# Sums moved from GpSimd to VectorE, and a later place for the solved blocks, in a decoder layer

## The chip, the core and the metric

The kernel runs on one core of a Trainium2 chip. Its time is the device time of one execution in microseconds (us); what counts is the median over several executions. The core has a matrix engine (TensorE, PE in the profile), an engine for elementwise work on two operands (VectorE, DVE), one for activations and casts (ScalarE, ACT), a slower one for elementwise work and for issuing transfers (GpSimd, POOL), and a queue of transfers without arithmetic (SyncE, SP). Every engine works off its own list of instructions in order, and waits on semaphores where an instruction needs something that another engine or a transfer has not finished.

## The reference

One decoder layer on 512 tokens of width 1024, in float32. In short:

```
u    = rmsnorm(x)
proj = u @ w_in                      # q, k, v, gates of two token mixers, two merge gates
ro   = silu(rgate) * groupnorm(retention(rq, rk, rv))         # 8 heads
do   = silu(dz) * rmsnorm(gated_delta(cq, ck, cv, g, beta))   # 8 heads, chunks of 128
         # inside: solve (I + A) sol = rhs, A strictly lower triangular, 128 x 128 per chunk and head
h    = x + (sigmoid(gate_r) * (ro @ w_ret_br) + sigmoid(gate_d) * (do @ w_dn_br)) @ w_o
up   = causal_depthwise_conv(rmsnorm(h) @ w_up)
out  = rmsnorm(h + (silu(a) * b) @ w_down)                    # a, b the halves of up
```

The result has to keep float32 accuracy.

## The kernel before

**Products.** TensorE multiplies rounded float32 operands fast. For full accuracy each operand is split into a high part (a cast) and a low part (the operand less its high part), and every product is three matmuls: high by high, high by low, low by high. A weight block is 128x1024: SyncE loads it into one of four raw buffers (`wraw`, `fetch()`), ScalarE casts it (`whi`), VectorE subtracts (`wlo`), and TensorE then works on both (`weights()`, `take()`). There are four buffers each of `whi` and `wlo`. A raw buffer is free, and the next load goes out, once its `wlo` is made.

**Stages.** First come the columns of `w_in` for the mixers (`dense_c` and others), and, among them, the two mixers themselves. Then four square products 512x1024 by 1024x1024, `matrix(0)` to `matrix(3)`: the merge gates of the delta branch (0) and of the retention branch (1), then the delta branch's output (2) and the retention branch's output (3). After them `w_o` (OUT), the upward product with its convolution, and the downward product. The square products and the downward one use a seven-product scheme in place of eight: each operand is cut into quarters B11, B12, B21, B22, and sums T1 to T4 of the quarters are made on chip. The weights' sums are made by transfers that add in memory, issued by GpSimd (`presum`, `s` in the profile), each released by a pair of tiny instructions, `tick` on ScalarE and `tock` on GpSimd (`pace()`). The sums for stage 3 and OUT are issued by `late_sums()`, which starts when the last head's solve is up. In a square stage one product is two weight blocks of 12 matmuls each, in PSUM as `py`.

**Sums and ends of a stage.** `combine_c` makes T3 and T1 on GpSimd and T2 and T4 on VectorE, in four rows of 128x256, for four column groups of each operand (`uy`, `uz`, `dy`, `dz`, `ry`, `rz`). `combine()`, which other operands use, makes all four on VectorE. `u_raw()` first puts u together again from its high and low part, eight sums of 128x512 (`ur`). `parts_of` and `part_of` split a sum into high and low (`oh`, `ol`, `o`). When a stage's tile of 128x512 is complete (`ended`), `branch_end` multiplies it with its gate: in stage 2 on GpSimd, in stage 3 on VectorE, followed by an addition of the two branches (`res<-res,res` in the profile). `m_out` then transposes the merged tile on TensorE (`pmt`, L219), ScalarE copies it out, and sums for OUT are made from it (`mt`, one of them on GpSimd, `mT` after the split). Ahead of `matrix(3)` SyncE issues eight loads of x (`h`, 256 KB each) for the residual.

**The solve.** For each of two groups of four heads, `solve(g)` inverts 32x32 blocks on VectorE, stores them and loads them back in another layout by transfers (`x_dram`, then `tt`), waits, and starts `solve_up`, whose first matmuls read `tt` (`pm`, 32x32).

**What sets the order.** There is no runtime scheduler. The program is written as generators, and an `Order` object keeps a model clock: every matmul moves the clock on by its planned cost, every instruction of another engine gets a planned end from a cost function, and a generator that yields n goes on n planned microseconds after its last instruction's planned end. `poll()`, called between products, issues whatever is due. So the yields and the cost functions decide the place of each instruction in its engine's list; the lists are fixed when the kernel is built. All VectorE, ScalarE and GpSimd rows are recorded at L200, matmuls at L215.

Of the kernel before, what the change touches and what calls it, by code (L numbers as in the profile page):

```python
# [11 lines left out]
F32 = mybir.dt.float32  # L12
F32R = mybir.dt.float32r
AF = mybir.ActivationFunctionType
ALU = mybir.AluOpType
# [40 lines left out]
HK = KT // 2  # L56
# [41 lines left out]
class Order:  # L98
# [29 lines left out]
    def spawn(self, gen, after=0.0):  # L128
        self.n += 1
        heapq.heappush(self.tasks, ((self.clock if self.now is None else self.now) + after, self.n, gen))  # L130
# [91 lines left out]
def body(nc, tc, ctx, io):  # L222
    sp = nc.sync
    order = Order()
    spawn, poll, hold = order.spawn, order.poll, order.hold
    vec = Engine(order, "vec", nc.vector, vec_cost)
    act = Engine(order, "act", nc.scalar, act_cost)
    pool = Engine(order, "pool", nc.gpsimd, pool_cost)
# [14 lines left out]
    def S(name, dt=F32):  # L243
        return heap.tile([P, T], dt, name=name, tag="s", bufs=HEAP)
# [17 lines left out]
    def ck(n, f=P):  # L262
        return slice(n * f, (n + 1) * f)
# [208 lines left out]
    def halves(a):  # L472
        return a[:, ck(0, 256)], a[:, ck(1, 256)]

    def combine(raw, k, nk, y, z):

        b11, b12 = halves(raw[k])
        b21, b22 = halves(raw[k + nk])
        (t3, t1), (t2, t4) = halves(y), halves(z)
        vec.tensor_tensor(t3, b22, b12, ALU.subtract)  # L480
        vec.scalar_tensor_tensor(t2, t3, -1.0, b11, ALU.mult, ALU.subtract)
        vec.tensor_tensor(t1, b11, b12, ALU.subtract)
        vec.scalar_tensor_tensor(t4, t2, -1.0, b21, ALU.mult, ALU.subtract)
# [47 lines left out]
    def transpose4(src, name):  # L531
        pt = PS(name)
        for n in range(NT):
            pe.transpose(pt[:, ck(n)], src[:, ck(n)], ident)
        return pt
# [62 lines left out]
    uhi = [S(f"uhi{k}", F32R) for k in range(KT)]  # L598
    ulo = [S(f"ulo{k}", F32R) for k in range(KT)]
    u = (uhi, ulo)  # L600
# [255 lines left out]
    def solve(g):  # L856

        group = heads[g * GH:(g + 1) * GH]
        while not all("k" in hd["got"] for hd in group):
            yield 0.3  # L860
        while g > 0 and not all("o" in hd["got"] for hd in heads[(g - 1) * GH:g * GH]):
            yield 0.3
        sa = [heap.tile([P, 32, 16], F32, name=f"sa{i}", tag="s", bufs=HEAP) for i in range(2)]
        adv = a_dram[g].rearrange("b h n i j -> (b h n) i j")
        for i in range(2):
            sp.dma_start(sa[i][:NP], adv[:, :, ck(i, 16)])
        xx = small.tile([P, 32, 32], F32, name="xx", tag="xx", bufs=1)
        tmp = small.tile([P, 32, 32], F32, name="xtmp", tag="xtmp", bufs=1)
        pool.memset(xx[:NP], 0.0)
        pool.memset(xx.rearrange("p a b -> p (a b)")[:NP, ::33], 1.0)  # L870
        yield 8.0
        for j in range(31):
            shp = [NP, j + 1, 31 - j]
            a = sa[j // 16][:NP, j + 1:, j % 16].unsqueeze(1).to_broadcast(shp)
            tv, xv_ = tmp[:NP, :j + 1, j + 1:], xx[:NP, :j + 1, j + 1:]
            vec.tensor_tensor(tv, a, xx[:NP, :j + 1, j:j + 1].to_broadcast(shp), ALU.mult)
            vec.tensor_tensor(xv_, xv_, tv, ALU.subtract)
            yield
        sp.dma_start(x_dram[g].rearrange("b h n i j -> (b h n) (i j)"), xx[:NP].rearrange("p a b -> p (a b)"))
        for b in range(4):  # L880
            sp.dma_start(tt_all[R32[b], :, R32[b]], x_dram[g][b].rearrange("h n j i -> j (h n) i"))
        yield 11.0
        for i, hd in enumerate(group):
            spawn(solve_up(hd, i), i * 4.0)

# [268 lines left out]
    dd, rr_, uu = ({} for _ in range(3))  # L1154
# [1 line left out]
    sums_of = {}  # L1156

    def combine_c(raw, x, c):

        y, z = S(f"{x}y{c}"), S(f"{x}z{c}")  # L1160
        b11, b12 = halves(raw[c])
        b21, b22 = halves(raw[c + HK])
        (t3, t1), (t2, t4) = halves(y), halves(z)
        pool.tensor_tensor(t3, b22, b12, ALU.subtract)
        yield
        pool.tensor_tensor(t1, b11, b12, ALU.subtract)
        vec.scalar_tensor_tensor(t2, t3, -1.0, b11, ALU.mult, ALU.subtract)
        vec.scalar_tensor_tensor(t4, t2, -1.0, b21, ALU.mult, ALU.subtract)
        yield
        sums_of[x, c] = y, z  # L1170

    def gate_out(ps, c, src, raw, x):
# [9 lines left out]
    def u_raw():  # L1182
        for k in (0, 4, 1, 5, 2, 6, 3, 7):
            uu[k] = S(f"ur{k}")
            pool.tensor_tensor(uu[k], uhi[k].bitcast(F32), ulo[k].bitcast(F32), ALU.add)
            yield 3.0
            if k >= HK:
                yield from combine_c(uu, "u", k - HK)

    for k in range(HK):  # L1190
        for i, (j, t) in (("B11", (0, 0)), ("B21", (1, 0)), ("B22", (1, 1))):
# [2 lines left out]
    def parts_of(opnd, names, src):  # L1194

        hi, lo = S("oh", F32R), S("ol", F32R)
        yield from split(hi, lo, src)
        for (name, k), h, l in zip(names, halves(hi), halves(lo)):
            opnd[name, k] = h, l

    def part_of(opnd, name, k, src):
        hi, lo = halves(S("o", F32R))
        yield from split(hi, lo, src)
        opnd[name, k] = hi, lo
# [3 lines left out]
    def operands_c(opnd, raw, x, gap, since):  # L1208

        if raw:  # L1210
            for c in range(HK):
                while now[0] < since[0] or c not in raw:
                    yield 0.5
                spawn(part_of(opnd, "B11", c, raw[c][:, ck(0, 256)]))
                yield gap
            for c in range(HK):
                while now[0] < since[1] or c + HK not in raw:
                    yield 0.5
                spawn(parts_of(opnd, (("B21", c), ("B22", c)), raw[c + HK]))
                spawn(combine_c(raw, x, c))  # L1220
                yield gap
        names = ("T3", "T1"), ("T2", "T4")
        for n, i in enumerate((1, 0)):
            for c in range(HK):
                while (x, c) not in sums_of or now[0] < since[2 + n]:
                    yield 0.5
                spawn(parts_of(opnd, [(name, c) for name in names[i]], sums_of[x, c][i]))
                yield gap
# [15 lines left out]
    def all_operands():  # L1244
        yield from operands_c(u_opnd, None, "u", 1.2, (0, 0, 0, 0))
        yield from operands_c(d_opnd, dd, "d", 2.0, (8, 9, 12, 13))

    spawn(all_operands())
    spawn(operands_c(r_opnd, rr_, "r", 2.0, (14, 15, 16, 17)))
    gates = [{}, {}]  # L1250
    merged = {}


    o_raw, o_opnd = {}, {}
# [4 lines left out]
    def o_split(name, t, src):  # L1259
        hi, lo = S(f"m{name}", F32R), S(f"m{name}", F32R)  # L1260
        yield from split(hi, lo, src)
        o_opnd[name, t] = hi, lo

    def m_out(t, i, r):
        yield 0.2
        pt = transpose4(r, "pmt")
        yield
        name, half = f"B{i + 1}{t // 2 + 1}", t % 2
        m = o_raw[name, half] = S(f"mr{t}{i}")
        act.copy(m, pt)  # L1270
        yield
        if name in ("B11", "B21", "B22"):
            spawn(o_split(name, half, m))
        if name == "B12":
            t3 = S("mt3")
            vec.tensor_tensor(t3, o_raw["B22", half], m, ALU.subtract)
            t2 = o_raw["T2", half] = S("mt2")
            vec.scalar_tensor_tensor(t2, t3, -1.0, o_raw["B11", half], ALU.mult, ALU.subtract)
            spawn(o_split("T2", half, t2), 0.2)
            yield 2.5  # L1280
            t1 = S("mt1")
            pool.tensor_tensor(t1, o_raw["B11", half], m, ALU.subtract)
            yield
            spawn(o_split("T1", half, t1), 0.2)
            yield 2.5
            spawn(o_split("T3", half, t3), 0.2)
        elif name == "B21":
            yield 1.5
            t4 = S("mt4")
            vec.scalar_tensor_tensor(t4, o_raw["T2", half], -1.0, m, ALU.mult, ALU.subtract)  # L1290
            spawn(o_split("T4", half, t4), 0.2)
# [9 lines left out]
    def branch_end(s, t, i, r, ps):  # L1301
        g = gates[s - 2].pop((t, i))
        if ps is None:
            (pool if s == 2 else vec).tensor_tensor(r, r, g, ALU.mult)
        else:
            vec.scalar_tensor_tensor(r, ps, -1.0, g, ALU.mult, ALU.mult)
        if s == 2:
            merged[t, i] = r
            return
        vec.tensor_tensor(r, r, merged.pop((t, i)), ALU.add)  # L1310
        yield
        yield from m_out(t, i, r)
# [330 lines left out]
```

## Time and profile before

| | before |
|---|---|
| median of 3 runs | 1029.83 us (1029.27 to 1030.21) |
| the profiled execution's own time | 1027.94 us |
| its span, first to last instruction | 1026.1 us |
| mean granted TensorE clock | 0.989 |
| TensorE busy | 991.8 us, 97% |
| VectorE busy | 737.7 us, 72% |
| ScalarE busy | 535.6 us, 52% |
| GpSimd busy | 213.9 us, 21% |

The busy shares are means over stages. What a stage is worth is read from its own stretch of the timeline, from the waits of TensorE that fall into it, and from the clock that was granted there (1.00 is full speed). Idle time on an engine other than TensorE costs nothing by itself. Stages 2 and 3 lie between about 490 and 620 us, the first group's solve ends at 186 us.

### The profile page before, as it was taken

What the parts mean: (1) busy time and instruction counts of PE and PEld (TensorE: products, weight loads), DVE (VectorE), ACT (ScalarE), POOL (GpSimd) and SP (SyncE); (2) the same over time, 40 slices, a digit from 0 to 9 for tenths busy, and PEclk for the clock granted to TensorE, in tenths of its full rate; (3) what the DMA queues carried; (4) which work ended last, traced back from release to release, by engine and by line L of the source; (5) the groups of instructions that cost most, each with busy time, mean ns of one, the idle gap of its engine ahead of it and who ended that gap; (6) DMA issues with size and microseconds to landing.
All of it is one profiled execution on the core that took longest, in us unless ns stands there. A gap on an engine that the chain in (4) does not pass through costs nothing.

```text
span 1026.1 us, 14395 instructions
## 1 busy us (share of the span) xinstructions
PE 991.8 (97%) x5241; PEld 823.5 (80%) x5241; DVE 737.7 (72%) x1332; ACT 535.6 (52%) x1132; POOL 213.9 (21%) x252
## 2 busy tenths in 40 slices
PE   8999999999999999999997979999999999999997
PEld 7888888687778887888885767788888888888886
DVE  5867797556677796565799669966555676778785
ACT  5699222278655322576675355654443443346664
POOL 3022112114333212442333301022112212000001
PEclk9999999999999999999999989999999999999999
DMA  7243559567668623359999863646669999346663
GB/s 260 83 141 117 156 184 232 164 189 148 170 202 175 157 94 115 104 181 272 346 275 244 236 208 124 224 154 219 235 213 194 212 204 218 101 125 193 202 185 123
DMA packets 82230, 189.29 MB, mean 184 GB/s; under 512 B 22704, under 2 KB 31216, under 8 KB 82160
## 3 DMA queue, kind: packets, MB, share of 16 engines
q1 hardware_dynamic: 54640, 123.36, 36.9%
q0 software_dynamic: 27520, 65.02, 28.6%
q8 instruction: 41, 0.67, 0.3%
q14 instruction: 29, 0.24, 0.1%
HBM read 185.17 MB, written 68.19 MB: 247 GB/s over the span
## 4 chain that ended last, share of the span: by engine, by line
PE 59%; DVE 8%; DMA 4%; ACT 3%; issue 2%; POOL 0%; POOLq 0%; DVEq 0%; ACTq 0%
PE pa L215 12%; PE pb L215 12%; PE pd L215 10%; PE pz L215 8%; PE py L215 5%; DVE wlo L200 3%; DMA wraw<-s 3%; PE pv L215 2%; PE po L215 2%; PE pq L215 2%; DMA wraw<-wm 2%; PE psc L215 1%; PE pk L215 1%; DVE res L200 1%; ACT whi L200 1%
## 5 line engine op out<-in xcount | busy, mean ns | idle before, releaser
L200 DVE TENSOR_TENSOR wlo<-wraw,whi 128x1024 fp32r<-128x1024 f32 x212 | 267.6, 1265 | 71.0 <-ACT whi L200 70.6
L200 ACT CAST whi<-wraw 128x1024 fp32r<-128x1024 f32 x212 | 219.4, 1035 | 163.4 <-PE pr L215 55.7
L200 POOL TENSOR_SCALAR tock<-tick 128x1 f32<-128x1 f32 x72 | 35.6, 495 | 356.1 <-ACT tick L200 356.0
L200 DVE SCALAR_TENSOR_TENSOR acc<-pb,prm,acc 128x511 f32<-128x511 f32 (+1 forms) x44 | 33.0, 749 | 57.2 <-ACT acc L200 56.4
L215 PE MATMUL pa<-u2lo,whi 128*128 128x512 f32 (+1 forms) x192 | 71.7, 373 | 1.8 <-DVE u2lo L200 1.8
L215 PE MATMUL pa<-u2hi,whi 128*128 128x512 f32 (+1 forms) x192 | 71.6, 373 | 0.0
L215 PE MATMUL pa<-u2hi,wlo 128*128 128x512 f32 (+1 forms) x192 | 71.4, 372 | 0.0
L215 PE MATMUL py<-wlo,oh 128*128 128x512 f32 x160 | 63.9, 399 | 7.2 <-DVE wlo L200 7.2
L215 PE MATMUL pb<-u2hi,whi 128*128 128x512 f32 (+1 forms) x184 | 70.0, 380 | 0.0
L215 PE MATMUL pb<-u2lo,whi 128*128 128x512 f32 (+1 forms) x184 | 70.0, 380 | 0.0
L215 PE MATMUL pb<-u2hi,wlo 128*128 128x512 f32 (+1 forms) x184 | 70.0, 380 | 0.0
L215 PE MATMUL py<-whi,oh 128*128 128x512 f32 x160 | 64.1, 401 | 0.0
L215 PE MATMUL py<-whi,ol 128*128 128x512 f32 x160 | 63.5, 397 | 0.0
L215 PE MATMUL pd<-whi,T 128*128 128x512 f32 (+1 forms) x198 | 55.5, 366 | 0.0
L215 PE MATMUL pz<-uhi,whi 128*128 128x512 f32 x128 | 52.5, 410 | 0.0
L215 PE MATMUL pr<-whi,uhi 128*128 128x512 f32 x128 | 52.1, 407 | 0.0
L215 PE MATMUL pr<-whi,ulo 128*128 128x512 f32 x128 | 50.8, 397 | 0.0
L215 PE MATMUL pr<-wlo,uhi 128*128 128x512 f32 x128 | 50.5, 394 | 0.0
L215 PE MATMUL pz<-uhi,wlo 128*128 128x512 f32 x128 | 50.0, 391 | 0.0
L215 PE MATMUL pz<-ulo,whi 128*128 128x512 f32 x128 | 50.0, 390 | 0.0
L200 DVE SCALAR_TENSOR_TENSOR acc<-pa,prm,acc 128x511 f32<-128x511 f32 (+1 forms) x44 | 33.0, 749 | 19.0 <-ACT acc L200 18.2
L215 PEld LDWEIGHTS pa<-u2lo,whi 128*128 128x128 f32 x192 | 36.2, 188 | 8.7 <-DVE u2lo L200 2.4
(320 smaller groups left out, 2498.9 us busy)
## 6 DMA issues: line engine op xcount, KB each, us to landing
wraw<-w SPq DMA_DIRECT2D x100, 512.0 KB, 4.5
s<-wm POOLq DMA_DIRECT2D x30, 1024.0 KB, 7.5
wraw<-s SPq DMA_DIRECT2D x60, 512.0 KB, 4.3
s<-wd POOLq DMA_DIRECT2D x24, 704.0 KB, 5.5
wraw<-wm SPq DMA_DIRECT2D x30, 512.0 KB, 4.5
s<-s POOLq DMA_DIRECT2D x10, 1024.0 KB, 11.2
wraw<-wd SPq DMA_DIRECT2D x15, 512.0 KB, 3.6
s<-s POOLq DMA_DIRECT2D x8, 704.0 KB, 9.4
```

What stands on the lines that cost most here:

```text
L200: return f(out, *args, **kw)
L215: self.engine.matmul(out, lhsT, rhs, start=start, stop=stop, **kw)
```

## The change

Five edits. The pause after the `tt` transfers of a solve is 13.5 planned us in place of 11.0. `combine_c` calls `combine()`, so that T3 and T1 are made on VectorE as well, and it is no longer a generator: its four rows are issued in one go. The sums of `u_raw`, one sum of `m_out` and the gating of stage 2 go to VectorE.

```diff
--- before.py
+++ after.py
@@ -879,7 +879,7 @@
         sp.dma_start(x_dram[g].rearrange("b h n i j -> (b h n) (i j)"), xx[:NP].rearrange("p a b -> p (a b)"))
         for b in range(4):
             sp.dma_start(tt_all[R32[b], :, R32[b]], x_dram[g][b].rearrange("h n j i -> j (h n) i"))
-        yield 11.0
+        yield 13.5
         for i, hd in enumerate(group):
             spawn(solve_up(hd, i), i * 4.0)
 
@@ -1156,17 +1156,8 @@
     sums_of = {}
 
     def combine_c(raw, x, c):
-
         y, z = S(f"{x}y{c}"), S(f"{x}z{c}")
-        b11, b12 = halves(raw[c])
-        b21, b22 = halves(raw[c + HK])
-        (t3, t1), (t2, t4) = halves(y), halves(z)
-        pool.tensor_tensor(t3, b22, b12, ALU.subtract)
-        yield
-        pool.tensor_tensor(t1, b11, b12, ALU.subtract)
-        vec.scalar_tensor_tensor(t2, t3, -1.0, b11, ALU.mult, ALU.subtract)
-        vec.scalar_tensor_tensor(t4, t2, -1.0, b21, ALU.mult, ALU.subtract)
-        yield
+        combine(raw, c, HK, y, z)
         sums_of[x, c] = y, z
 
     def gate_out(ps, c, src, raw, x):
@@ -1182,10 +1173,11 @@
     def u_raw():
         for k in (0, 4, 1, 5, 2, 6, 3, 7):
             uu[k] = S(f"ur{k}")
-            pool.tensor_tensor(uu[k], uhi[k].bitcast(F32), ulo[k].bitcast(F32), ALU.add)
+            vec.tensor_tensor(uu[k], uhi[k].bitcast(F32), ulo[k].bitcast(F32), ALU.add)
             yield 3.0
             if k >= HK:
-                yield from combine_c(uu, "u", k - HK)
+                combine_c(uu, "u", k - HK)
+                yield 1.0
 
     for k in range(HK):
         for i, (j, t) in (("B11", (0, 0)), ("B21", (1, 0)), ("B22", (1, 1))):
@@ -1217,7 +1209,7 @@
                 while now[0] < since[1] or c + HK not in raw:
                     yield 0.5
                 spawn(parts_of(opnd, (("B21", c), ("B22", c)), raw[c + HK]))
-                spawn(combine_c(raw, x, c))
+                combine_c(raw, x, c)
                 yield gap
         names = ("T3", "T1"), ("T2", "T4")
         for n, i in enumerate((1, 0)):
@@ -1279,8 +1271,7 @@
             spawn(o_split("T2", half, t2), 0.2)
             yield 2.5
             t1 = S("mt1")
-            pool.tensor_tensor(t1, o_raw["B11", half], m, ALU.subtract)
-            yield
+            vec.tensor_tensor(t1, o_raw["B11", half], m, ALU.subtract)
             spawn(o_split("T1", half, t1), 0.2)
             yield 2.5
             spawn(o_split("T3", half, t3), 0.2)
@@ -1301,7 +1292,7 @@
     def branch_end(s, t, i, r, ps):
         g = gates[s - 2].pop((t, i))
         if ps is None:
-            (pool if s == 2 else vec).tensor_tensor(r, r, g, ALU.mult)
+            vec.tensor_tensor(r, r, g, ALU.mult)
         else:
             vec.scalar_tensor_tensor(r, ps, -1.0, g, ALU.mult, ALU.mult)
         if s == 2:
```

Because every generator's due time follows from planned ends, rows elsewhere move too. GpSimd's list goes from 242 to 202 rows, VectorE's from 1166 to 1212. Three places:

TensorE's list at the first solved blocks. `pr` is the weight block's product with u, `pm` the first matmuls that read `tt`. Before:

```order
L215 MATMUL pr_1847<-whi_1800,ulo4_166 128x512
L215 MATMUL pm0_1940<-tt_178,A0_630 32x32 x8
L215 MATMUL pr_1847<-whi_1800,uhi5_159 128x512
L215 MATMUL pr_1847<-wlo_1809,uhi5_159 128x512
L215 MATMUL pr_1847<-whi_1800,ulo5_167 128x512
```

In the change, from the same row on:

```order
L215 MATMUL pr_1847<-whi_1800,ulo4_166 128x512
L215 MATMUL pr_1847<-whi_1800,uhi5_159 128x512
L215 MATMUL pr_1847<-wlo_1809,uhi5_159 128x512
L215 MATMUL pr_1847<-whi_1800,ulo5_167 128x512
L215 MATMUL pr_1848<-whi_1800,uhi4_158 128x512
L215 MATMUL pr_1848<-wlo_1809,uhi4_158 128x512
L215 MATMUL pr_1848<-whi_1800,ulo4_166 128x512
L215 MATMUL pr_1848<-whi_1800,uhi5_159 128x512
L215 MATMUL pr_1848<-wlo_1809,uhi5_159 128x512
L215 MATMUL pr_1848<-whi_1800,ulo5_167 128x512
L215 MATMUL pm0_1951<-tt_178,A0_630 32x32 x8
```

Nine `pr` matmuls that stood behind the first `pm` now stand ahead of it.

VectorE's list in stage 3, where the sums of the retention operand (`ry`, `rz`) and the gating rows of stage 2 (`res<-res,res`) are made. Before, with `rz` alone of the four sums, the others being in GpSimd's list:

```order
L200 SCALAR_TENSOR_TENSOR rz_5592<-rz_5592,r_3871 128x256
L200 TENSOR_TENSOR wlo<-wraw,whi 128x1024
L200 TENSOR_TENSOR ol<-r_3871,oh 128x512
L200 TENSOR_TENSOR res_5563<-res_5563,py 128x512
L200 TENSOR_TENSOR ol<-r_3913,oh 128x512
L200 SCALAR_TENSOR_TENSOR rz_5613<-ry_5612,r_3740 128x256
L200 SCALAR_TENSOR_TENSOR rz_5613<-rz_5613,r_3913 128x256
L200 TENSOR_TENSOR res_5568<-res_5568,py 128x512
L200 TENSOR_TENSOR wlo<-wraw,whi 128x1024
```

In the change:

```order
L200 TENSOR_TENSOR wlo<-wraw,whi 128x1024
L200 TENSOR_TENSOR ol<-r_3873,oh 128x512
L200 TENSOR_TENSOR res_5557<-res_5557,py 128x512
L200 TENSOR_TENSOR res_5563<-res_5563,py 128x512
L200 TENSOR_TENSOR ry_5621<-r_3913,r_3742 128x256
L200 SCALAR_TENSOR_TENSOR rz_5622<-ry_5621,r_3742 128x256
L200 TENSOR_TENSOR ry_5621<-r_3742 128x256
L200 SCALAR_TENSOR_TENSOR rz_5622<-rz_5622,r_3913 128x256
L200 TENSOR_TENSOR wlo<-wraw,whi 128x1024
L200 TENSOR_TENSOR res_5557<-res_5557,res_4820 128x512
L200 TENSOR_TENSOR ol<-r_3913,oh 128x512
L200 TENSOR_TENSOR res_5563<-res_5563,res_4829 128x512
```

Four `ry` and `rz` rows now stand together between two `wlo`, and the gating rows `res<-res,res` stand in this list.

SyncE's list at the eight loads of x. `s_3` are stage 3's weight sums (L282), `h` the loads of x, whose line is L1357 before and L1348 in the change. Before:

```order
L282 DMA wraw<-s_3_91 128x1024 x2
L1357 DMA h_00_5885<-x 128x512
L1357 DMA h_01_5887<-x 128x512
L1357 DMA h_10_5889<-x 128x512
L1357 DMA h_11_5891<-x 128x512
L1357 DMA h_20_5893<-x 128x512
L1357 DMA h_21_5895<-x 128x512
L1357 DMA h_30_5897<-x 128x512
L1357 DMA h_31_5899<-x 128x512
L282 DMA wraw<-s_3_89 128x1024 x2
```

In the change:

```order
L282 DMA wraw<-s_3_91 128x1024 x2
L282 DMA wraw<-s_3_89 128x1024
L1348 DMA h_00_5872<-x 128x512
L1348 DMA h_01_5874<-x 128x512
L1348 DMA h_10_5876<-x 128x512
L1348 DMA h_11_5878<-x 128x512
L1348 DMA h_20_5880<-x 128x512
L1348 DMA h_21_5882<-x 128x512
L1348 DMA h_30_5884<-x 128x512
L1348 DMA h_31_5886<-x 128x512
L282 DMA wraw<-s_3_89 128x1024
```

One half of `s_3_89` is now issued ahead of the eight loads; before, both halves stood behind them.

## The prediction

> **What bounds the kernel now.** I read the busy times first, then the waits of TensorE, to see which few waits are worth money.
>
> ```profile
> PE 991.8 (97%) x5241; PEld 823.5 (80%) x5241; DVE 737.7 (72%) x1332; ACT 535.6 (52%) x1132; POOL 213.9 (21%) x252
> PE pmt L219 <- DVE res L200: 8.8, 1, 8.8
> PE py L215 <- DVE wlo L200: 7.2, 2, 5.5
> PE pm L215 <- DMA tt<-x_dram: 2.5, 1, 2.5
> PE po L215 <- DVE mT L200: 1.3, 1, 1.3
> ```
>
> TensorE sets the end. The change takes no matmul away, so all that it can bring lies in TensorE's idle time and in the half clock that follows it. The first three waits add to 18.5 us; each is touched. Next the stretches in which they lie: PE, PE weight load, VectorE, ScalarE and GpSimd busy in us (with instructions), then granted clock, DMA share, GB/s.
>
> ```profile
> 494.00:520.00 26.00, 26.00 (x116) 21.38 (x115) 23.79 (x29) 17.84 (x30) 11.87 (x14) 1.00 1.00 343
> 520.00:546.00 26.00, 24.33 (x107) 19.57 (x105) 23.89 (x29) 20.44 (x36) 7.90 (x10) 1.00 0.99 261
> 546.00:572.00 26.00, 20.48 (x84) 16.50 (x83) 25.90 (x28) 13.88 (x20) 9.43 (x9) 0.93 0.77 222
> 572.00:598.00 26.00, 17.24 (x76) 14.12 (x75) 14.76 (x16) 7.67 (x9) 5.94 (x4) 0.85 0.87 262
> ```
>
> In the first three VectorE is 92 to 99% busy; there it is the bound, not TensorE. A share of busy time does not say that it works, though. Around the longest wlo wait, from the timelines:
>
> ```profile
> 553.04 0.79 PE L215 MATMUL py<-wlo,oh 128*128 128x512 f32 x1 [5.52 <-DVE wlo L200]
> 547.60 0.68 DVE L200 TENSOR_TENSOR res<-res,py 128x512 f32<-128x512 f32 x1
> 548.20 4.79 DVE L200 TENSOR_TENSOR wlo<-wraw,whi 128x1024 fp32r<-128x1024 f32 x1
> 548.08 1.24 POOL L200 TENSOR_TENSOR ry<-r 128x256 f32<-128x256 f32 x1
> 549.45 1.76 POOL L200 TENSOR_TENSOR res<-res,res 128x512 f32<-128x512 f32 x1
> 550.67 1.22 POOL L200 TENSOR_TENSOR ry<-r 128x256 f32<-128x256 f32 x1
> 540.44 1.04 ACT L200 CAST whi<-wraw 128x1024 fp32r<-128x1024 f32 x1 [0.16 <-DMA wraw<-s]
> ```
>
> The subtraction that makes wlo takes 4.79 us here and 1.23 in a quiet place (592.66, below). It ends when GpSimd's run of sums ends (550.67 + 1.22 = 551.9) plus about one quiet wlo. Its whi was there from 541.48. So TensorE waits for a VectorE row that GpSimd's rows hold up.
>
> **Part 1, the moved sums.** In 489 to 578 us the groups of VectorE are (count, then busy and mean ns); the last two rows are groups of the whole span, the price of a plain 128x256 and 128x512 sum:
>
> ```profile
> L200 DVE TENSOR_TENSOR wlo<-wraw,whi 128x1024 fp32r<-128x1024 f32 x29 | 48.1, 1665 | 7.9 <-ACT whi L200 7.8
> L200 DVE SCALAR_TENSOR_TENSOR rz<-ry,r 128x256 f32<-128x256 f32 x4 | 2.8, 688 | 0.0
> L200 DVE SCALAR_TENSOR_TENSOR rz<-rz,r 128x256 f32<-128x256 f32 x4 | 1.7, 425 | 0.1
> L200 DVE TENSOR_TENSOR ol<-rz,oh 128x512 fp32r<-128x512 f32 x4 | 2.7, 684 | 0.0
> L200 DVE TENSOR_TENSOR res<-res,res 128x512 f32<-128x512 f32 x14 | 10.5, 758 | 0.5
> L200 DVE TENSOR_TENSOR y<-r,r 128x256 f32<-128x256 f32 x11 | 4.7, 425 | 0.3
> ```
>
> Added to VectorE there: the sums of both branches' operands, 2 x 4 x 2 = 16 rows of 128x256 at 0.425 us (6.8), and 6 gating rows at 0.758 (4.5): 11.3 us. Taken off: the stretch of 29 wlo, 29 x (1.665 - 1.23) = 12.6 us, and of rz beside its quiet twin, 4 x (0.688 - 0.425) = 1.1: 13.7 us. VectorE gets some 2.4 us lighter, and what counts more, no wlo is held for 4.79 us.
>
> The new order could still pile rows up. The worst run of the change (VectorE's rows shown with the diff begin it) goes over four weight blocks: four wlo at 1.23, three groups of four sums at 1.7, one o at 0.42, two ol at 0.68, two res out of PSUM at 0.68, two gating rows at 0.758, together 4.9 + 5.1 + 0.4 + 1.4 + 1.4 + 1.5 = 14.7 us. A block is 12 matmuls, by 520 to 546 us 24.33 / 107 = 0.227 each, so 2.72, and four are 10.9. VectorE falls back by 3.8 us. The cover: the whi of the late block was ready at 541.48, its matmul was wanted at 553.04 - 5.52 = 547.52, so a quiet wlo has 6.04 - 1.23 = 4.8 us to spare. 3.8 fits into 4.8, with a single us over. I cost it at nothing; were a weight load late by more than that us, up to half of these waits would stay (rival C).
>
> What the waits cost now: 7.2 us of idle time, and the half clock behind the longer one:
>
> ```profile
> 553.00:556.00 3.00, 2.96 (x7) 2.38 (x8) 2.97 (x5) 1.51 (x3) 0.00 (x0) 0.50 1.10 250
> 598.00:600.00 2.00, 2.00 (x7) 1.52 (x6) 1.97 (x4) 0.82 (x2) 0.00 (x0) 0.50 0.65 190
> 600.00:602.00 2.00, 2.00 (x11) 1.69 (x10) 0.61 (x3) 1.08 (x2) 0.00 (x0) 0.85 0.61 201
> 188.00:190.00 2.00, 2.00 (x6) 1.58 (x5) 0.06 (x1) 0.00 (x0) 0.00 (x0) 0.50 0.85 350
> 190.00:192.00 2.00, 2.00 (x37) 1.22 (x37) 0.12 (x1) 0.51 (x2) 0.00 (x0) 0.75 0.10 37
> ```
>
> From the first row 2.96 x 0.5 = 1.5 us. Term: **-8.7 us** (bounds: 0 if the stretch has another cause, -8.7 if all goes).
>
> **Part 2, the solved blocks.** The 2.5 us wait for tt is followed by half clock: 2 x 0.5 + 2 x 0.25 = 1.5 us in the last two rows. It costs 4.0 us in all. In the change nine matmuls more stand ahead of the first pm (the order shown above): 9 x 0.227 = 2.05 us. What remains is 2.49 - 2.05 = 0.45 us, and I take it that so short a wait leaves the clock alone: **-3.5 us** (bounds: -2.05 if the clock falls all the same, -4.0 if the data come a little sooner).
>
> The Trainium skill ("TensorE: Matmul & The Clock Gate", section "What's actually happening") has the clock halved only after a whole idle window of about 3.4 us. By that rule a 2.5 us wait would cost no clock, and this term would be 2.05 us and not 3.5. The 0.50 granted at 188 to 190 us, behind 2.49 us of idle, speaks against it, so the row is taken.
>
> Queued behind the nine matmuls is only pr work that needs no solved block, so nothing waits for it longer than before. The second group of heads gets the same 2.5 us; TensorE did not wait for it, so nothing.
>
> **Part 3, the longest wait.** The chain of waits across it, and SyncE's queue:
>
> ```profile
> 578.05 1.08 DVE wlo L200
> 579.13 12.36 DMA wraw<-s
> 591.58 1.05 ACT whi L200
> 592.66 1.23 DVE wlo L200
> 593.89 1.81 DVE res L200 x3
> 595.72 0.70 DVE res L200
> 596.46 1.11 PE pmt L219 x4
> 574.65 0.33 SPq L282 DMA_DIRECT2D wraw<-s  x1
> 575.07 3.91 SPq L1357 DMA_DIRECT2D h<-x  x8
> ```
>
> VectorE's res rows for pmt stand behind the wlo of one weight block, whose 0.5 MB were asked for at 579.13, right after eight loads of h (2 MB), and landed 12.4 us later. No engine is slow here; a transfer is queued behind another. It costs 8.76 us, and half clock: 596.46 to 598 as in 598 to 600, 0.8, then 1.0 and 2 x 0.15 = 0.3: 10.8 us.
>
> By the new order one weight block more (s_3_89, its first half) goes ahead of the h loads and the next behind them. The first pmt is free then, but the second stands behind the next block's wlo in VectorE's queue. Count from the start of the block that was being multiplied when the load was asked for: the first pmt was wanted at 596.46 - 8.76 = 587.70, by TensorE's count 3.25 blocks later, so the start lies at 587.70 - 3.25 x 2.72 = 578.86, and the second, before the block after, is wanted at +11.2. Its load lands, by bytes, when the block ahead (0.5), h (2) and itself (0.5) have gone at the 262 GB/s of 572 to 598 us: 3.15 MB / 0.262 = 12.0, so at +12.3; or, by the row, 12.36 behind an issue at one block later, +15.4. Then whi 1.05, wlo 1.23 and two res 1.4: ready at +16.1 to +19.1, middle +17.6. Wait 6.4, and 2.1 of half clock as now: 8.5 against 10.8, **-2.3 us** (bounds: 0, the same wait one block on, and -10.8, if the load lands in time; below zero is unlikely since the load goes out no later after its block than now). I take the middle, since the h loads stay ahead of a block that the chain needs.
>
> **Small parts.**
>
> ```profile
> 625.74 3.00 POOL L200 TENSOR_TENSOR mt<-mr,mr 128x512 f32<-128x512 f32 x2 [47.55 <-ACT mr L200]
> L200 POOL TENSOR_TENSOR ur<-uhi,ulo 128x512 f32<-128x512 f32 x8 | 12.2, 1530 | 43.0 <-issue 14.2 <-DVE r L200 10.7 <-DVE d L200 7.5
> 364.00:390.00 26.00, 26.00 (x116) 21.53 (x116) 22.56 (x42) 7.62 (x10) 6.90 (x4) 1.00 0.32 95
> ```
>
> The two mt sums are 2 x 0.758 = 1.5 us more on VectorE, in the stretch where po waits 1.3 us for mT; the splits that follow no longer wait for GpSimd's 1.5 us a row. From 0 to +1.5, taken **+0.3**, nearer to the gain since the chain through them gets shorter. The eight ur sums (6.1 us on VectorE) and the eight sums behind them (3.4) fall around 364 to 390 us, where VectorE is 22.6 of 26 busy under a TensorE that never stops; their cover is that work for stage 0, which is not due before its blocks come. Taken at 0, up to +1.5 without the cover.
>
> **Sum.** -8.7 - 3.5 - 2.3 + 0.3 = -14.2 us. The profiled execution took 1027.94 us (its span is 1026.1), so 1013.7; the median of the runs stands 1.89 above it (1029.83), so **1015.6 us**.
>
> **Rivals.** B, the h loads do no harm any more: part 3 gives all of its 10.8. For it: 12.3 us by bytes is already close, and each us that VectorE gains upstream sends the loads out sooner. Against: three more us of whi, wlo and res stand behind the landing. 8.5 us better: 1007.1.
>
> C, weights still bind in 494 to 578 us: DMA engines are at 1.00 and 0.99 in two of its windows, and only 1 us of cover was over. With half of part 1 left (4.4) and the clock falling at tt anyway (1.5): 1021.5.
>
> D, slower: the stretch of wlo is not GpSimd's doing but that of the busy DMA, or comes back from GpSimd's remaining work. Then VectorE simply gets more. In 520 to 578 us it has 2.1 + 0.1 us free under TensorE and gets 3.4 + 4.5 = 7.9: 5.7 us; from the d sums (3.4 on 2.2 free) 1.2; half clock 1.5: +8.4, less 3.5 at tt, so 1034.7. It decides as soon as less than 11.3 of the 13.7 us go: wlo's mean in that stretch would stay above 1.665 - 10.2/29 = 1.31 us. Against: the 4.79 us row ends with GpSimd's run, and the res row out of PSUM beside it keeps 0.68. The Trainium skill ("SBUF — State Buffer", section "SBUF: two separate sides") says that a VectorE row with two inputs in SBUF and a GpSimd row that reads SBUF shut each other out for a whole instruction. By that rule D falls; no run here has shown it by itself, so I keep a small chance.
>
> E, it does not do what it says: the waits move. The first pm meets its data as late as now, or a new queue on VectorE eats what GpSimd's rows gave back: about 1029.
>
> **How the numbers follow.** Forecast 0.50, B 0.20, C 0.20, D 0.05, E 0.05. Faster: the first three, 0.90. Same, within 0.2% or 2 us, about what a measurement of this kernel can tell: 0.05. Slower: 0.05. The range runs from just under B to just over C, 1006 to 1023; D and E are left out.
>
> **What would show it.** In the profile after: wlo in the stretch of 489 to 578 us at a mean near 1.25 and not above 1.31; no py wait for wlo, no half clock before the pmt; pm waiting for tt under 0.6 us at full clock; pmt's wait shorter, 4 to 9 us, and behind the wlo of a load issued after the h loads. Wrong if wlo keeps rows of 3 to 5 us with GpSimd idle, if py waits go on with short wlo (then it is the load or the pile on VectorE), or if pmt does not wait at all, which is B.

## The result and the profile after

| | before | after |
|---|---|---|
| median | 1029.55 us (1027.77 to 1030.21, 4 runs) | 1022.88 us (1021.29 to 1023.93, 4 runs) |
| the profiled execution's own time | 1027.94 us | 1023.75 us |
| its span | 1026.1 us | 1022.0 us |
| GpSimd busy | 213.9 us | 166.0 us |
| VectorE busy | 737.7 us | 734.0 us |

The ratio is 0.9937, with an interval of 0.9917 to 0.9957: faster by 6.7 us. Forecast were 14.2. More than half of the gain is missing. The two profiled executions lie only 4.2 us apart: the one before was 1.6 us faster than its median, the one after 0.9 us slower.

VectorE took on 40 rows more, those that left GpSimd (1332 to 1372 in the profile; the list counts of 1166 and 1212 given with the change lie six too far apart), and is less busy than before. The mean of wlo in the stretch of stages 1 to 3, forecast near 1.25 us, is 1.221. The group of wlo in 489 to 578 us, then a piece of VectorE's timeline in stage 3 (start and duration in us):

```profile
L200 DVE TENSOR_TENSOR wlo<-wraw,whi 128x1024 fp32r<-128x1024 f32 x33 | 40.2, 1221 | 9.9 <-ACT whi L200 9.8
548.56 1.22 DVE L200 TENSOR_TENSOR wlo<-wraw,whi 128x1024 fp32r<-128x1024 f32 x1
549.70 0.42 DVE L200 TENSOR_TENSOR ry<-r,r 128x256 f32<-128x256 f32 x1
550.15 0.42 DVE L200 SCALAR_TENSOR_TENSOR rz<-ry,r 128x256 f32<-128x256 f32 x1
550.49 0.42 DVE L200 TENSOR_TENSOR ry<-r 128x256 f32<-128x256 f32 x1
550.83 0.42 DVE L200 SCALAR_TENSOR_TENSOR rz<-rz,r 128x256 f32<-128x256 f32 x1
551.16 1.22 DVE L200 TENSOR_TENSOR wlo<-wraw,whi 128x1024 fp32r<-128x1024 f32 x1
```

wlo falls from 1665 to 1221 ns in the mean, none takes longer than 1.23 us where the longest took 4.87, and the four sums cost 1.7 us together, as priced. The waits of TensorE and its stretches (columns as in the prediction):

```profile
PE pmt L219 <- DVE res L200: 6.5, 1, 6.5
PE psc L215 <- ACT vn L200: 6.5, 1, 6.5
PE po L215 <- DVE mT L200: 2.2, 2, 1.2
182.00:208.00 26.00, 25.99 (x257) 19.58 (x256) 15.06 (x36) 7.21 (x21) 4.38 (x6) 1.00 0.68 201
208.00:234.00 26.00, 19.53 (x144) 17.07 (x142) 10.50 (x29) 14.76 (x52) 2.66 (x4) 0.91 0.39 122
520.00:546.00 26.00, 26.00 (x116) 21.56 (x115) 24.95 (x39) 21.16 (x37) 4.03 (x6) 1.00 0.99 324
546.00:572.00 26.00, 26.00 (x116) 21.52 (x116) 24.38 (x36) 17.47 (x25) 1.75 (x2) 1.00 1.03 292
572.00:598.00 26.00, 19.48 (x81) 15.79 (x80) 16.80 (x21) 10.40 (x15) 1.48 (x2) 0.87 0.88 267
```

Three things are to be seen. The waits for wlo are gone: 520 to 572 us is full, at full clock. The wait for tt is gone too, with its half clock (182 to 208 us). But a wait of 6.5 us that was not there stands in 208 to 234 us: psc for vn. It is in the delta rule's scan of the first group of heads, the work right behind the solve. Its cause, row by row (TensorE, then ScalarE, VectorE and GpSimd):

```profile
223.98 0.38 PE L215 MATMUL psc<-Sn,k 128*128 128x128 f32 x2
230.84 0.80 PE L215 MATMUL psc<-vn,ktok 128*128 128x128 f32 x2 [6.47 <-ACT vn L200]
219.95 0.25 ACT L200 COPY vn<-psc 128x128 f32<-128x128 f32 x1
224.40 0.28 ACT L200 ACTIVATE A<-pkt 128x128 f32<-128x128 f32 x1 [4.20 <-PE psc L215]
228.79 1.15 ACT L200 ACTIVATE ktok<-pkt,ekd 128x128 f32<-128x128 f32 x4 [3.25 <-DVE R L200]
230.54 0.41 ACT L200 COPY vn<-psc 128x128 f32<-128x128 f32 x2
225.58 0.17 DVE L200 TENSOR_SCALAR ssk<-ssk 128x4 f32<-128x4 f32 x1 [4.97 <-ACT A L200]
227.38 1.12 DVE L200 SCALAR_TENSOR_TENSOR A<-pkk,sr,gb 128x128 f32<-128x128 f32 x4
228.42 0.34 DVE L200 SCALAR_TENSOR_TENSOR R<-psc,c,vtok 128x128 f32<-128x128 f32 x1
225.83 1.04 POOL L200 TENSOR_TENSOR rk<-ssk,mhalf 128x4 f32<-128x4 f32 x1 [7.78 <-DVE ssk L200]
```

ScalarE's A and ktok, VectorE's ssk and A, and GpSimd's rk belong to the first head of the second group (`k_front`). They stand ahead of rows R (VectorE) and vn (ScalarE) of the first group's scan. A waits 4.2 us for a psc of the first group; then A, ssk, rk, A and R run one after the other through three engines, ktok waits for R, and vn stands behind ktok. TensorE takes its list in order and has to wait with it. Why A needs that psc the trace does not show; the tiles of one pool are handed on in turn, so A may take over one that the scan still reads. That fits the rows: A starts as the psc that reads `k` ends, and ktok as R ends, which reads `vtok`. But it is argued, not shown.

Before, the same A stood elsewhere. Its row on ScalarE and the first row of the product that it hangs on (`pk`), before, then that product's row in the change:

```profile
233.99 0.28 ACT L200 ACTIVATE A<-pkt 128x128 f32<-128x128 f32 x1 [0.59 <-PE pkt L219]
205.41 0.50 PE L215 MATMUL pk<-uhi,whi 128*128 128x512 f32 x1
197.94 0.50 PE L215 MATMUL pk<-uhi,whi 128*128 128x512 f32 x1
```

Behind the first pm stood 39 `pr` matmuls before; now nine of them are done ahead of it and 30 are left, so the product behind them comes sooner. `pk` starts 7.5 us earlier and A 9.6 us earlier, while the scan's first psc starts as before (198.73 and 198.66). This work of the second group moved forward past the scan. Of the scan's 16 copies vn, 13 stood ahead of this A in ScalarE's list before, 7 do now; of its 12 rows R, 10 stood ahead of VectorE's A, 5 do now.

The clock behind the wait, in windows of 2 us:

```profile
230.00:232.00 2.00, 1.16 (x5) 1.17 (x6) 0.00 (x0) 1.22 (x6) 0.00 (x0) 0.50 0.12 17
234.00:236.00 2.00, 2.00 (x10) 1.58 (x7) 0.86 (x3) 1.08 (x6) 0.00 (x0) 0.50 0.00 0
236.00:238.00 2.00, 2.00 (x17) 1.59 (x16) 0.61 (x2) 1.06 (x6) 1.30 (x2) 0.97 0.00 0
```

From 230.84 to 236 the clock is half (0.50 in 232 to 234 too): 5.16 x 0.5 = 2.6 us. With the 6.5 us of wait this costs 9.1 us, more than the 4.0 that the wait for tt had cost.

The chain of waits over pmt after the change:

```profile
572.94 3.93 DMA h<-x
576.94 12.64 DMA wraw<-s
589.67 1.05 ACT whi L200
590.75 1.23 DVE wlo L200
593.36 1.11 PE pmt L219 x4
```

It is the chain of before, one weight block on: a load behind the eight loads of x takes 12.6 us.

The account between the two profiled executions: waits for wlo -8.7, tt -4.0, vn +9.1, pmt -2.3 (its half clock is alike in both), po +0.9, and +1.5 in the first 26 us (the loads and sums of the start; TensorE's busy time there lies between 20.8 and 22.6 us in all runs below, though the edits come later, so it is not put down to the change). That is -3.5 of the -4.1 us of the spans.

### The profile page after: what moved, and what is told of

Same layout as the page of the kernel before. It is cut to its first block, busy times and chain, and to the rows that moved or that the text cites. A ratio compares the mean times of both kernels' runs of the same rounds, so it can differ in the third digit from the quotient of the medians.

```text
span 1022.0 us, 14344 instructions
## 1 busy us (share of the span) xinstructions
PE 992.4 (97%) x5241; PEld 825.0 (81%) x5241; DVE 734.0 (72%) x1372; ACT 535.2 (52%) x1130; POOL 166.0 (16%) x212
## 4 chain that ended last, share of the span: by engine, by line
PE 84%; DVE 8%; DMA 3%; issue 2%; ACT 2%; POOL 0%; SPq 0%; POOLq 0%; ACTq 0%; DVEq 0%
PE pa L215 12%; PE pb L215 12%; PE pd L215 10%; PE py L215 9%; PE pz L215 9%; PE pr L215 9%; PE pk L215 5%; PE pv L215 4%; PE pq L215 4%; PE psc L215 3%; DVE wlo L200 2%; DVE res L200 2%; PE pm L215 2%; PE po L215 1%; PE pro L215 1%
## 5 line engine op out<-in xcount | busy, mean ns | idle before, releaser
L200 DVE TENSOR_TENSOR wlo<-wraw,whi 128x1024 fp32r<-128x1024 f32 x212 | 254.6, 1202 | 70.7 <-ACT whi L200 67.8
L200 POOL TENSOR_SCALAR tock<-tick 128x1 f32<-128x1 f32 x72 | 31.4, 436 | 461.5 <-ACT tick L200 461.4
L215 PEld LDWEIGHTS pa<-u2hi,whi 128*128 128x128 f32 x192 | 36.9, 192 | 7.6 <-ACT u2hi L200 1.4
```

What stands on the lines that cost most here:

```text
L200: return f(out, *args, **kw)
L215: self.engine.matmul(out, lhsT, rhs, start=start, stop=stop, **kw)
```

## The experiments

Each ratio is to the kernel before, run again beside the experiment (medians of 1029.1 to 1030.0 us).

**The pause alone, on the kernel before.**

```diff
-        yield 11.0
+        yield 13.5
```

> The kernel before with the longer pause alone (13.5 in place of 11.0). Theory: the pause moves all rows of the delta rule behind the first solve, so that TensorE's wait for tt goes (2.5 us and 1.5 us of half clock, -4.0), and in its place a wait of TensorE for vn opens near 230 us (6.5 us and some 2.3 us of half clock, +8.8): about 1034 us, slower than before. Rival: the wait for vn belongs to the moved sums or to that execution; then the pause alone gives about 1026 us, with no wait of psc above 2 us.

1033.2 us (1032.2 to 1033.8), ratio 1.0035, interval 1.0022 to 1.0048. The waits:

```profile
PE pmt L219 <- DVE res L200: 9.3, 1, 9.3
PE psc L215 <- ACT vn L200: 6.5, 1, 6.5
PE py L215 <- DVE wlo L200: 5.8, 4, 3.6
```

The wait for vn is there, as long as in the change, without one moved sum. No wait for tt is among the first seven. The longer pause by itself makes the kernel slower.

**The pause taken back, the moved sums kept.** The change with the diff above reversed.

> The changed kernel with the pause back at 11.0, all moved sums kept. Theory: TensorE waits 2.5 us for tt again, but no longer 6.5 us for vn, so about 1018 us, 5 us faster than the change. Rival: the wait for vn stays and the one for tt comes back, about 1027 us.

1017.05 us (1015.9 to 1019.6), ratio 0.9876, interval 0.9858 to 0.9894. Waits:

```profile
PE pmt L219 <- DVE res L200: 7.5, 1, 7.5
PE pm L215 <- DMA tt<-x_dram: 2.7, 1, 2.7
```

tt is back, vn gone. Against the change this is 5.8 us less; the two waits' prices give 9.1 - 4.0 = 5.1. So the moved sums alone are worth 12 us, and the pause takes 5 to 6 back. The rival of both runs falls.

**GpSimd busy, but not reading.** The kernel before, in which GpSimd leaves out the sums T3 and T1 and the gating of stage 2 and, in their place, writes zeros over the same tiles, after a read of 128x1 that keeps the order:

```diff
+    def fill(out, src, n):
+        order.issue("pool", pool_cost("tensor_tensor", out.shape[-1], 0, None))
+        nc.gpsimd.tensor_scalar(out[:, :1], src[:, :1], 1.0, None, ALU.mult)
+        for _ in range(n):
+            nc.gpsimd.memset(out[:, 1:], 0.0)
-        pool.tensor_tensor(t3, b22, b12, ALU.subtract)
+        fill(t3, b22, 3)
...
```

and the same for T1 and the gating of stage 2.

> The kernel before, in which GpSimd does not add or multiply in the operand sums T3 and T1 and in the gating of stage 2, but writes zeros over the same tiles for about as long (one read of 128x1 to keep the dependence, then three fills); the sums and the gating are left out. The order of all rows stays. Theory, that a GpSimd row which reads SBUF shuts out a VectorE row with two inputs in SBUF: no wlo above 1.5 us beside the fills, mean wlo in the stretch of stages 1 to 3 about 1.25 us, the two waits of py for wlo gone, about 1029.5 - 9 = 1020 us. Rival, that it is GpSimd's mere being busy, the transfers, or the order in which VectorE waits for GpSimd's sums: wlo keeps a mean near 1.6 us and rows of 3 to 5 us, py waits 5 us or more, 1027 to 1031 us.

1014.28 us, with an unusually wide spread (1006.9 to 1017.4), ratio 0.9842, interval 0.9800 to 0.9884. That is 6 us below the expected 1020; why is not shown, and since this kernel multiplies zeros, its time carries no weight here. Its rows do. Groups of GpSimd and VectorE in 489 to 578 us, then a wlo beside a fill:

```profile
L1162 POOL MEMSET res<- 128x511 f32 x18 | 9.5, 525 | 0.7
L200 DVE TENSOR_TENSOR wlo<-wraw,whi 128x1024 fp32r<-128x1024 f32 x32 | 38.9, 1221 | 11.5 <-ACT whi L200 11.3
548.26 1.70 POOL L1162 MEMSET res<- 128x511 f32 x3
548.98 1.22 DVE L200 TENSOR_TENSOR wlo<-wraw,whi 128x1024 fp32r<-128x1024 f32 x1
PE pmt L219 <- DVE res L200: 6.8, 1, 6.8
```

GpSimd is busier than with its sums (14.1 us of 520 to 546 us against 7.9), in the same place of the lists, and wlo keeps 1.22 us; the longest takes 1.23. Being busy is not what stretches wlo, nor are the transfers (DMA share 1.03, 1.04, 0.90 in the three windows of 494 to 572 us); the wide sums of GpSimd are. The fills write the same tiles, so what is left is that the sums read whole tiles. That agrees with the rule of the Trainium skill cited in rival D ("SBUF — State Buffer", section "SBUF: two separate sides"), which speaks of a GpSimd row that reads SBUF. What happens to a VectorE row with one such input no run here was made for. The last row matters below: the wait of pmt is 6.8 us here, with the loads of x standing where they stood before.

**One half of the moved work each.** The gating of stage 2 alone, and the operand sums T3 and T1 alone, on the kernel before:

```diff
-            (pool if s == 2 else vec).tensor_tensor(r, r, g, ALU.mult)
+            vec.tensor_tensor(r, r, g, ALU.mult)
```

> The kernel before with the gating of stage 2 alone moved to VectorE. Theory (every GpSimd row that reads SBUF holds up wlo for its own length): the operand sums still stretch wlo, so some of the two waits of py stays, 2 to 5 of 7.2 us, pmt's wait of 8 to 9 us stays, about 1025 us. Rival, that the gating rows alone made the waits: none left, 1020 us.

> The kernel before with the operand sums T3 and T1 alone moved to VectorE (the gating, the sums of u and the one of mt stay on GpSimd). Theory: 32 rows of GpSimd go, of them 16 in stages 1 to 3; wlo is stretched by the six gating rows alone, the waits of py for wlo fall from 7.2 to under 2 us, and with one weight block ahead of the loads of x the wait of pmt falls by 2 us: 1019 to 1021 us. Rival, that the gating rows matter as much: 4 us of py's wait left, 1024 us.

Gating alone: 1025.3 us (1024.5 to 1027.2), ratio 0.9960, interval 0.9947 to 0.9974. Operand sums alone: 1020.7 us (1020.3 to 1021.4), ratio 0.9909, interval 0.9890 to 0.9929. wlo in 489 to 578 us, in this order, and the wait of the first:

```profile
L200 DVE TENSOR_TENSOR wlo<-wraw,whi 128x1024 fp32r<-128x1024 f32 x30 | 43.3, 1446 | 8.7 <-ACT whi L200 7.1 <-PE py L215 1.5
PE py L215 <- DVE wlo L200: 5.5, 2, 3.8
L200 DVE TENSOR_TENSOR wlo<-wraw,whi 128x1024 fp32r<-128x1024 f32 x33 | 41.6, 1264 | 10.4 <-ACT whi L200 10.4
```

16 rows of 128x256 hold up wlo more than 6 rows of 128x512. With the operand sums gone no wait for wlo is left among the longest; with the gating gone 5.5 of 7.2 us are, a little above the expected 2 to 5. The longest wlo agrees: 4.86 us with the operand sums left on GpSimd, 2.01 us with the gating left there. The operand sums alone met their expected time, but the wait of pmt fell by 1.0 us there and not by 2.

**The loads of x later.** On the change, and the same with the pause at 11.0:

```diff
-            for t in range(NT):
-                for i in range(2):
-                    h1[t][i] = S(f"h1_{t}{i}")
-                    sp.dma_start(h1[t][i], xv[t, :, ck(i, T)])
+            spawn(h_loads())
...
+    def h_loads():
+        while now[0] < len(PRODUCTS) * 3 + 4:
+            yield 0.5
+        for t in range(NT):
+            for i in range(2):
+                h1[t][i] = S(f"h1_{t}{i}")
+                sp.dma_start(h1[t][i], xv[t, :, ck(i, T)])
+                yield 1.4
```

> The changed kernel with the eight loads of x issued one by one from the fifth product of stage 3 on, behind the weight loads that pmt's rows need. Theory: the weight block of the second pmt is loaded in some 5 us, the wait of pmt (6.5 us and about 2 us of half clock) goes, and nothing else waits for x: about 1014.5 us. Rival: the block is late because of GpSimd's weight sums or the busy DMA, then a wait of 4 us or more is left: 1019 us or above.

> The changed kernel with the pause back at 11.0 and the eight loads of x issued later (both edits of the two runs before together). If the two waits are independent, the gains add: 1022.9 - 5.8 - 6.8 = 1010.3 us, with a wait of 2.5 us for tt left and none of pmt above 1 us. Rival, that they share time (the shifted order brings pmt's wait back, or the load of the solve's results shifts): 1013 us or above.

1016.1 us (1013.6 to 1018.4), ratio 0.9870, interval 0.9848 to 0.9892, and 1010.9 us (1008.7 to 1012.2), ratio 0.9811, interval 0.9787 to 0.9836. In the first no wait of pmt is among the seven longest. In the second one is left; its wait, the GpSimd transfer that adds weights in memory, and the load in its chain:

```profile
PE pmt L219 <- DVE res L200: 2.1, 1, 2.1
566.34 1.27 POOL L200 DMA_DIRECT2D s<-s  x1
569.27 9.96 DMA wraw<-s
```

No load of x is in SyncE's list ahead of that weight load, and it takes 10 us all the same. It was asked for 2.9 us behind the last weight sum of 1 MB. That points to this sum as a second, smaller cause beside the loads of x; the runs with that sum sooner, below, test it. The two gains add: 1010.3 us were expected of both edits together.

**The front of the next head later.** The change with the loads of x later, and in `k_front`, ahead of A:

```diff
+        if h == GH:
+            yield 7.0
         A = hd["A"] = S(f"A{h}")
```

> The changed kernel with its pause of 13.5 kept, the loads of x later, and the first head of the second group held by 7 planned us ahead of its rows A and ktok on ScalarE, so that they and the sums that hang on them stand behind the rows vn and R of the first group's scan and not ahead of them. Theory: TensorE's 6.5 us wait for vn was the rows A and ktok standing ahead of vn in ScalarE's list; it goes with its 2 us of half clock, and no wait for tt comes back: 1016.1 - 8 = 1008 us, 2 us better than with the pause at 11.0. Rival, that the scan itself is late with the longer pause, or that another row takes the place: a wait of 3 us or more is left or opens in 200 to 290 us, 1012 us or above.

1011.8 us (1010.9 to 1015.5), ratio 0.9834, interval 0.9805 to 0.9863: 4.3 us less than without the hold, where 8 were expected. The longest waits that are new:

```profile
PE pkv L215 <- DVE ro L200: 2.7, 1, 2.7
PE pot L219 <- ACT vn L200: 1.2, 1, 1.2
```

The 6.5 us for vn are gone, so the place of A and ktok in the lists made them. 2.7 and 1.2 us open elsewhere in the same stretch, which comes close to the rival, and 2 us at pmt. The longer pause was not made worth its price by this: with the pause at 11.0 and the same loads the time was 1010.9 us.

**What sets the length of pmt's wait.** The prediction had it that one weight block more ahead of the loads of x shortens it. On the change, the loads issued one block earlier again:

```diff
...
+        while now[0] < len(PRODUCTS) * 2 + 6:
+            yield 0.5
+        yield 3.0
...
```

> The changed kernel with the eight loads of x issued one weight block earlier, ahead of both halves of s_3_89 as in the kernel before. Theory of the prediction (the wait of pmt falls because one block more goes ahead of the loads): the wait rises again by about 2 us, 1025 us. Rival, that the wait is set by how many bytes stand ahead and when, and comes out alike on either side: 6 to 7 us of wait, 1022 to 1024 us.

1019.2 us (1017.9 to 1023.1), ratio 0.9914, interval 0.9886 to 0.9941:

```profile
PE pmt L219 <- DVE res L200: 4.2, 1, 4.2
```

Both expectations miss. The wait gets shorter by 2.3 us, not longer; the time lies 3.7 us lower, though with runs that overlap those of the change. With the fills (loads in the old place, 6.8 us) and with the operand sums alone (loads in the new place, 7.8 us in two waits) this says that the block ahead of the loads is not what shortened the wait. What did is not settled. That the loads of x make most of the wait is shown by the run with the loads later.

**The last weight sum sooner.** On the change; then with the loads later and the pause at 11.0; then that with the pause at 12.0:

```diff
-        yield from presums((3, OUT), 1, (c, c + 125.0, 15), (c + 140.0, c + 140.0, 1))
+        yield from presums((3, OUT), 1, (c, c + 125.0, 15), (c + 128.0, c + 128.0, 1))
```

> The changed kernel with the last of GpSimd's weight sums (a transfer that adds 1 MB in memory) released 12 planned us earlier, so that it does not run beside the loads of x. Theory, that pmt's weight block waits for the bytes of both, x and that sum: the load lands some 4 us sooner (1 MB at 262 GB/s), the wait falls from 6.5 to 2 to 4 us: 1019 us. Rival, that the loads of x alone do it: the wait stays above 6 us, 1023 us.

> The moved sums with the pause at 11.0, the loads of x later and the last weight sum 12 planned us earlier. If that sum's transfer is what is left of pmt's wait (2.1 us and some 1.5 us of half clock), 1007 to 1008 us. Rival, that the sum now delays weight blocks of stages 2 and 3: waits of py for wlo or whi of 2 us or more, 1010 us or above.

> As the run before, with the pause at 12.0: the first pm stands 3 matmuls (0.7 us) later than with 11.0. If only the place of the first pm counted, the wait for tt would be 1.8 us and the time 0.7 to 1 us shorter than in the run before. Rival: rows A and ktok of the second group come to stand elsewhere once more, and a wait for vn or R of 2 us or more opens, so that it is 2 us longer or more.

Alone 1022.0 us (1021.1 to 1022.8), ratio 0.9934, interval 0.9914 to 0.9954: the change's own time. GpSimd's row and the wait:

```profile
572.36 1.27 POOL L200 DMA_DIRECT2D s<-s  x1 [5.52 <-DMA s<-s]
PE pmt L219 <- DVE res L200: 6.4, 1, 6.4
```

The sum waits 5.5 us for the one before it and so starts only 2 us sooner than in the change (574.35). The run does not part the two theories.

All three: 1008.8 us (1007.0 to 1009.8), ratio 0.9804, interval 0.9783 to 0.9825; with the pause at 12.0 1007.05 us (1004.7 to 1011.5), ratio 0.9796, interval 0.9759 to 0.9833. The waits for tt in the one and the other, and pmt's in the other:

```profile
PE pm L215 <- DMA tt<-x_dram: 3.2, 2, 2.6
PE pm L215 <- DMA tt<-x_dram: 1.8, 2, 1.0
PE pmt L219 <- DVE res L200: 1.2, 1, 1.2
```

With the first, pmt's wait is 1.0 us in place of the 2.1 without the edit: the sum starts 3.5 us sooner (562.83 against 566.34), and the weight load takes 7.4 us in place of 10.0. So the sum was part of that wait. At 12.0 the wait for tt is 1.4 us shorter and none for vn opens, but the two times cannot be told apart. The second group's A comes at 240.40 us there, behind 14 of the 16 vn: at pauses of 11.0, 12.0 and 13.5 it stands behind 13, 14 and 7, so its place does not follow the pause in one direction. Both beat the change by 14 to 16 us and the kernel before by about 2%.

## Why the prediction was wrong

The time fell into the range, by 0.1 us and by luck, since its upper end was set for rival C; the gain was less than half of the forecast. By its steps:

- **Part 1, the moved sums: right.** wlo at 1.22 us, no wait for wlo, -8.7 us as summed. One reading was off without harm: VectorE was not the bound in 494 to 520 us, where TensorE was busy for all of its 26.00 us. The worst pile of rows on VectorE left no wait, as the 3.8 against 4.8 us had it. The cause is shown by the fills and the two halves, so rival D falls. Kept alone, the sums gave 12 us where the terms of parts 1 and 3 and of the small parts make 10.7.
- **Part 2, the pause: wrong.** The term itself, tt, came out: -4.0 where -3.5 was taken. That no wait at all was left is luck: in the run with the last weight sum sooner, whose pause is the same, 1.3 us of it are left. The step that failed is the sentence "Queued behind the nine matmuls is only pr work that needs no solved block, so nothing waits for it longer than before." It looked at TensorE's list at one place, and at what waits for the nine matmuls, not at what they let go ahead. With them done before the first pm, the pr work ended sooner, and the product behind it, `pk` of the second group's first head, came 7.5 us earlier while the scan did not. So that head's A and ktok came to stand ahead of rows R and vn of the scan that had stood ahead of them, and TensorE waited 6.5 us and ran at half clock for 5.2. In place of -3.5 the part is +5.1 by the waits, about +4 us on the kernel before and +5.8 on top of the sums.
- **Part 3, pmt: right in size by luck, not in its reason.** Forecast 6.4 us of wait, measured 6.5, behind a load issued after the loads of x. The reason given, one block more ahead of the loads, is contradicted by the loads put one block earlier (4.2 us) and by the fills (6.8 us in the old place).
- **Small parts: right in size.** po +0.9 against +0.3; no wait came from the sums of u.
- **The rivals.** E said "the waits move", and had the mechanism by its name, but at no place and no price, and so a chance of 0.05. C's time, 1021.5, is near the measured one for another reason: weights did not bind. The list of what would prove the forecast wrong had no row for the scan.

## What to carry to other kernels

Where a table of due times sets all lists, a later place for one piece of work is an earlier place for other work. Price such an edit on every engine as far as the moved work reaches, and look for rows of other work with their own waits that now stand ahead of it. Two edits of one change are best run apart: here one gave 12 us and the other took 5 to 6 back.

A busy share near 100% can be another engine's work. If a row of one form takes 1.2 us in one place and 4.8 in another, look what runs beside the long one before the row itself is made cheaper.

## What the runs showed of the hardware

- Three fills of GpSimd, 1.7 us, beside a wlo of 1.22 us: only GpSimd's reading sums stretched it (4.79 us).
- More rows made VectorE less busy: it ran 1372 in place of 1332, and its busy time went from 737.7 to 734.0 us. The time for which it is shut out is shown as the length of its own rows.
- The clock fell to half after a wait of 2.49 us (tt, before) and stayed at half for 5 us behind one of 6.47 us, but it stayed full behind a wait of 1.3 us for tt (the run with the last weight sum sooner) and behind one of 1.67 us for wlo (before, 541 to 544 us). Two waits of 1.04 and 0.77 us close together halved it as well (the run with the pause at 12.0, 0.50 in 188 to 190 us). The window of 3.4 us that the Trainium skill names ("TensorE: Matmul & The Clock Gate", section "What's actually happening") is longer than the wait of 2.49 us that halved the clock here.
